# Weight sums moved from GpSimd to VectorE, and a source-ordered attention, in a one-layer transformer kernel

## Chip, cores and metric

The kernel runs as one program on 1 core of one Trainium2 chip. The metric is the device time of one execution in microseconds (us). Engines are named as in the profile: PE (TensorE matmul), PEld (its weight loads), DVE (VectorE), ACT (ScalarE), POOL (GpSimd), SP (SyncE, which here issues most DMAs).

## What is computed

One layer (DEPTH = 1), 2048 tokens, width 1024, 16 heads of 64, a feed-forward width of 2816, all in float32. Cut to what matters:

```python
def chunk_relpos_attention(h, w_qkv, w_o, rel_bias):       # chunks of 64 tokens
    q, k, v = split_heads(h, w_qkv)
    for c in range(n_chunks):                              # keys: own chunk and the 8 before it
        sc = einsum('bhqd,bhkd->bhqk', q_blk, k[:, :, k0:k1]) * scale + bias
        p = softmax(sc)
        outs.append(einsum('bhqk,bhkd->bhqd', p, v[:, :, k0:k1]))
    return merge_heads(concatenate(outs)) @ w_o

def reference(x, ...):
    h = rms_norm(x, g_pre_mix);  m = chunk_relpos_attention(h, w_qkv, w_o, rel_bias)
    x = x + rms_norm(m, g_post_mix)
    h = rms_norm(x, g_pre_ffn)
    return x + rms_norm((silu(h @ w_gate) * (h @ w_up)) @ w_down, g_post_ffn)
```

## The kernel before

**Split products.** Every large product is made of three matmuls (`products`, L185 to L187): both factors are split into a high part, copied by ACT (L131, L341), and a low remainder, subtracted by DVE (L132, L342), and hi*hi, hi*lo and lo*hi are summed in PSUM. Each weight tile (128x1024) thus costs one ACT copy and one DVE subtraction before TensorE can use it.

**Seven products for eight.** Values, queries and keys, gate and up, and down multiply 2x2 blocks with seven block products (B11, B21, T1, T2, B22, T3, T4). Four of them need sums of weight blocks, S1 to S4. For the first of two groups of 1024 tokens the kernel forms these sums itself: `sum_` in `block_items` adds two raw weight tiles in place (L834) and stores the sum in DRAM (L835) for the second group. There are 68 such adds: 8 for the values and 16 for queries and keys in the first 290 us, 44 for gate and up after 1217 us. (The sums for the down projection are made by DMA alone, L773, behind them on POOL's queue.)

**Stages.** `project` makes values, then queries and keys, for group 0 and then group 1, after some warm-up matmuls on an identity tile (L1256). The attention follows, then the last quarter of the output projection, then gate/up and down for both groups.

**Attention.** Tokens go in four quarters of 512; in each, eight pairs of heads; in each pair, four blocks of 128 queries. One block is a slot `t` (0 to 127). The first quarter has no earlier keys (`prev` false, up to 4 key blocks); in the others a block reads five key blocks (640 keys). Slot `t` emits, in this order: if it starts a pair, `output` of the pair before (`po`, L558, then its split, L341 and L342); `transposed(t)` (for either head four PE transposes into a PSUM tile `tt`, L528, copied to `pT` by DVE for head 0, L531, and by ACT for head 1, L533); `ahead(t + 3)`, the scores three slots ahead (L493, L494 into the single PSUM tile `st`, then per head a DVE reduction with the bias, L502, and an ACT exponential, L506; then a DVE reciprocal, L510, and a POOL scaling, L513); `fill`, some steps of the output projection of the quarter before; and `fifth` (two PE transposes for the fifth key block, L542, and one ACT copy for both heads, L543). The tag `tt` has two buffers, and a slot with earlier keys takes three of them: head 0, head 1, fifth.

**Output projection.** `o_quarter` takes 256 columns of `w_o` at a time, a slab of two weight tiles. `take` fetches slabs (`fetch`: DMA and split at once), one ahead. A result is copied by ACT (`y`, L582) into a tile of the ring `io` (three buffers) and stored; its squares are summed (L252, L253).

**Side work.** `later` is a queue of small steps; `tick` runs some after each product step, by due costs. `behind(w, n, lag, load, use)` spreads n loads and uses, each use `lag` steps behind its load. It serves the sums of squares and the residual writes (`write`, L1125, L1128; loads into `io` and the ring `sc`).

**Order.** PE issues in source order everywhere (`manual_schedule`). The order on ACT, DVE, POOL and SP is made by the planner of the tile framework from the source's order and expected times.

Of the kernel before, what the change touches and what calls it, by code (L numbers as in the profile page):

```python
# [9 lines left out]
F32 = mybir.dt.float32  # L10
# [39 lines left out]
def trunk(  # L50
# [79 lines left out]
    def split_part(hi, lo, raw):  # L130
        act.activation(hi, raw, AF.Copy)  # L131
        dve.tensor_tensor(lo, raw, hi.bitcast(F32), op=ALU.subtract)  # L132

    def fetch():
        n = len(ready)
        if n == len(plan):
            return
        tiles = [w_tile(f"{n}_{c}") for c in range(2)]
        for c in range(2):
            here = slice(c * 1024, c * 1024 + 1024)  # L140
            if "fp" in phase:
                part = phase["fp"].tile([P, 1024], F32, tag="w4", name=f"raw_{n}_{c}", bufs=phase["w4"])
            else:
                part = phase["ap"].tile([P, 1024], F32, tag="raw", name=f"raw_{n}_{c}", bufs=2)
            sp.dma_start(part, plan[n][:, here])
            split_part(*tiles[c], part)
        ready.append(tiles)

    taken = [0]

# [13 lines left out]
        def lo(self, k, c=slice(0, 256)):  # L164
            return self.part(1, k, c)

    def take(ahead=True):

        n = taken[0]
        taken[0] += 1  # L170
        if len(ready) == n:
            fetch()
        if ahead:
            fetch()
        return Slab(ready[n])

    def dense_bank(n):
# [254 lines left out]
    class Attend:  # L432
# [45 lines left out]
        def scores(self, ib):  # L478
# [17 lines left out]
            for h in range(2):  # L496
                c0 = cuts[h][0]
                sc = ap.tile([P, 640], F32, tag="sc", name="sc", bufs=8)
                nmax = rows[:, 4 + h : 5 + h]
                t = self.bias[h]  # L500
                rev = t[:, n - 1 :: -1] if n == 640 else t[:, 0:n][:, ::-1]
                dve.tensor_tensor_reduce(  # L502
                    out=sc[:, :n], in0=st[:, c0 : c0 + n], in1=rev, scale=-1.0, scalar=3.0e38,
                    op0=ALU.add, op1=ALU.min, accum_out=nmax,
                )
                act.activation(  # L506
                    sc[:, :n], sc[:, :n], AF.Exp, bias=nmax, scale=-1.0, accum_out=rows[:, h : h + 1]
                )
                self.sc[ib, h] = sc
            dve.reciprocal(rows[:, 2:4], rows[:, 0:2])  # L510
            for h in range(2):
                sc = self.sc[ib, h]
# [32 lines left out]
        def output(self):  # L545
            n, p = self.n, self.p
            v = values[n, p // 2]
            terms = [(0, 4, 0, HALF)]
            for r in range(1, 5 if self.prev else 4):
                if self.prev:  # L550
                    terms.append((r, r - 1, 0, r * P))
                if r < 4:
                    terms.append((r, 4 + r, r * P, HALF))
            po = phase["psa"].tile([P, HALF], F32, tag="po", name="po", bufs=1)
            for m, (r, kb, c0, c1) in enumerate(terms):
                for h in range(2):
                    c = (p % 2) * P + h * 64
                    pe.matmul(  # L558
                        po[heads[h], c0:c1], v[:, kb, c : c + 64], self.pT[:, h, r, c0:c1],
                        start=m == 0, stop=m == len(terms) - 1,  # L560
                    )
            if p == 0:
                ats[n] = Cols(((0, 1), (2, 3))[n % 2])
            split(ats[n].hi(p), ats[n].lo(p), po)

    def o_quarter(n):

# [3 lines left out]
        for d2 in range(KT // 2):  # L571
# [3 lines left out]
            for dt in (2 * d2, 2 * d2 + 1):  # L575
                pt = dense_bank(dt)
                c = slice((dt % 2) * P, (dt % 2) * P + P)
                for k in range(KT):
                    products(pt, w.hi(k, c), w.lo(k, c), src.hi(k), src.lo(k), k == 0, k == KT - 1)
                    yield 3 * C512  # L580
                t = io("y")
                act.activation(t, pt, AF.Copy)  # L582
                sp.dma_start(o_d[n][:, dt, :], t)
# [2 lines left out]
    class Blocks:  # L586
# [8 lines left out]
        def sums(self, w, on_all=False):  # L595
# [4 lines left out]
            for t in range(2):  # L600
# [11 lines left out]
                        self.total = nrm_tile("total")  # L612
                    add_square(c.pop(k), self.total, k == 0)

                steps += behind(w, KT, 1, load, use)
                if on_all:
                    steps.append((0.0, lambda t=t: later.extendleft(reversed(root_steps(self.rows[t], 1.5)))))
                    continue
# [204 lines left out]
    def block_items(src, key, early=True, ahead=None):  # L823
# [7 lines left out]
                sp.dma_start(r[a], src[BLOCK_AT[a]])  # L831

        def sum_(name, to, a, b, op=ALU.add):
            pool.tensor_tensor(r[to], r[a], r[b], op=op)  # L834
            last_pool[0] = pool.dma_start(sums_d[key][name], r[to])  # L835

        def make(n):
# [246 lines left out]
    class Late:  # L1084
# [5 lines left out]
        def sums(self, w):  # L1090
# [8 lines left out]
                    self.total = nrm_tile("total")  # L1099
                add_square(c.pop(dt), self.total, dt == 0)  # L1100

            return behind(w, KT, 1, load, use)

        def rstd(self, wait):
            return [(0.0, lambda: later.extendleft(reversed(root_steps(self.total, wait))))]
# [9 lines left out]
        def write(self, w, eng=dve):  # L1115
# [12 lines left out]
                eng.tensor_tensor(y, res, y, op=ALU.add)  # L1128
                sp.dma_start(self.dst[:, dt, :], y)

            return behind(w, KT, 1, load, use)


    rs, rows_of = [], {}
# [117 lines left out]
    def project():  # L1252

        warm = ps.tile([P, HALF], F32, tag="mm", name="warm")
        for _ in range(9):
            pe.matmul(warm[:, 0:P], ident, ident, start=True, stop=True)  # L1256
        groups = [Blocks([x[2 * g + t] for t in range(2)], PRE_MIX, SLOTS[g]) for g in range(NG)]
        for g in range(NG):
# [260 lines left out]
    def ahead(t):  # L1519
        if t < slots:  # L1520
            jobs[t // 4].scores(t % 4)
            if t % 4 == 1 and t // 4 + 1 < len(jobs):
                jobs[t // 4 + 1].load()

    for t in range(AHEAD):
        ahead(t)
    for t in range(slots):
        share = (0.4 if t % 4 == 0 else 1.2) * left[0] / max(per - t % per - 1, 1)
        if t > 0 and t % 4 == 0:
            fill(0.45 * share)  # L1530
            jobs[t // 4 - 1].output()
            if t % per == 0:
                n = t // per - 1
                fill(1e9)
# [3 lines left out]
                    later.extend(lates[n - 1].rows(1.5) + lates[n - 1].write(3.0, pool))  # L1538
                if n == 2:
                    later.extend(blocks[0].sums(2.0))  # L1540
        job = jobs[t // 4]
        job.transposed(t % 4)
        ahead(t + AHEAD)
        fill((0.55 if t % 4 == 0 else 1.0) * share)
        job.fifth()
    jobs[-1].output()
    fill(1e9)
    drain()
    for _ in sums_:
        pass  # L1550
    stack_a.close()
# [87 lines left out]
```

## Time and profile before

| | |
|---|---|
| median of 3 runs | 2501.5 us (2500.98 to 2511.96) |
| the profiled execution | 2506.22 us, its span 2504.4 us |
| mean granted TensorE clock | 0.982 |
| busy: PE, DVE, ACT, POOL | 94%, 67%, 46%, 20% of the span |
| instructions | 33018 |

The profile describes one execution. The span runs from its first to its last instruction; times in rows are microseconds from the span's start. A busy share is a mean over stages with different limits. An entry such as "[0.37 <-DVE rows L502]" says that the engine was idle for 0.37 us before the instruction, and that DVE's write of `rows` at line 502 ended the wait.

### The profile page before, as it was taken

The numbers are of one execution on the slowest core, as the hardware profiler recorded it, in microseconds if no ns is written. First come the engines' busy times: TensorE is split into PE (matmuls) and PEld (weight loads), VectorE is DVE, ScalarE is ACT, GpSimd is POOL, SyncE is SP. The second block draws the span as 40 slices with busy tenths as digits, with TensorE's granted clock in tenths as the row PEclk, the third lists the DMA queues.
The fourth block names the chain that finished last, engine by engine and source line by source line (L and its number), as shares of the span: only waits on it lengthen the run. The fifth ranks groups of instructions, "written<-read, shape, count | busy, mean of one in ns | idle before, by whom it ended". The sixth has DMA issues, their size and how long they took to land.

```text
span 2504.4 us, 33018 instructions
## 1 busy us (share of the span) xinstructions
PE 2360.5 (94%) x11442; PEld 1914.6 (76%) x11442; DVE 1672.8 (67%) x2557; ACT 1162.8 (46%) x2039; POOL 498.2 (20%) x490
## 2 busy tenths in 40 slices
PE   7899999978888899898999999999999999999998
PEld 6677788856666677666888878888888888888887
DVE  8768856556555565566977687676657657555567
ACT  6443743346555565565532333355443333334454
POOL 4223012123332433431433233300000000000002
PEclk8999999989999999999999999999999999999999
DMA  6466789999767877784576654457765755547654
GB/s 252 161 228 215 250 240 325 298 240 258 215 169 194 244 201 204 227 230 156 185 249 222 219 180 156 151 202 226 235 237 170 249 182 190 175 146 246 193 188 153
DMA packets 229783, 529.73 MB, mean 212 GB/s; under 512 B 26320, under 2 KB 42720, under 8 KB 225136
## 3 DMA queue, kind: packets, MB, share of 16 engines
q1 hardware_dynamic: 217712, 480.42, 60.9%
q0 software_dynamic: 11904, 47.19, 6.2%
q8 instruction: 91, 1.49, 0.3%
q14 instruction: 76, 0.62, 0.1%
HBM read 380.14 MB, written 170.44 MB: 220 GB/s over the span
## 4 chain that ended last, share of the span: by engine, by line
PE 54%; DVE 2%; ACT 1%; issue 1%; DMA 0%; POOL 0%; DVEq 0%; SPq 0%; ACTq 0%
PE pd L187 6%; PE pd L185 6%; PE pd L186 6%; PE pb L186 4%; PE pb L187 4%; PE pb L185 4%; PE pc L186 3%; PE pc L187 3%; PE pc L185 3%; PE pa L185 3%; PE pa L186 3%; PE pa L187 3%; PE po L558 1%; PE mm L187 1%; PE mm L185 1%; PE mm L186 1%
## 5 line engine op out<-in xcount | busy, mean ns | idle before, releaser
L513 POOL TENSOR_SCALAR sc<-sc,rows 128x640 f32<-128x640 f32 (+4 forms) x256 | 194.7, 773 | 399.7 <-DVE rows L510 197.7
L834 POOL TENSOR_TENSOR raw<-raw,raw 128x1024 f32<-128x1024 f32 x68 | 179.9, 2646 | 394.3 <-DMA raw<-in_w_gu 139.6
L506 ACT ACTIVATE sc<-sc,rows 128x640 f32<-128x640 f32 (+4 forms) x256 | 192.9, 755 | 112.6 <-DVE rows L502 112.4
L502 DVE CUSTOM_DVE_ANT_0 sc<-st,bias 128x640 f32<-128x640 f32 (+2 forms) x248 | 176.0, 746 | 86.0 <-PE st L494 60.4
L185 PE MATMUL pb<-hb,w_wg_T 128*128 128x512 f32 x528 | 205.6, 389 | 0.0
L187 PE MATMUL pb<-hb,w_wg_T 128*128 128x512 f32 x528 | 205.4, 389 | 0.0
L186 PE MATMUL pb<-hb,w_wg_T 128*128 128x512 f32 x528 | 205.4, 389 | 0.0
L528 PE MATMUL tt<-ident,sc 128*128 128x128 f32 x928 | 140.6, 281 | 45.6 <-DVE pT L531 21.5
L277 POOL TENSOR_TENSOR rs<-ms,neg_half 128x4 f32<-128x4 f32 (+1 forms) x7 | 7.9, 1125 | 854.8 <-DVE ms L275 854.8
L528 PEld LDWEIGHTS tt<-ident,sc 128*128 128x128 f32 x928 | 105.0, 143 | 82.2 <-issue 72.1
L493 PE MATMUL st<-k,q 128*128 128x384 f32 (+3 forms) x440 | 140.7, 340 | 28.0 <-DVE rows L502 23.1
L187 PE MATMUL pd<-a,w_d_T 128*128 128x512 f32 (+1 forms) x368 | 139.8, 380 | 0.1
L185 PE MATMUL pa<-hb,w_wg_B 128*128 128x512 f32 x352 | 137.7, 391 | 2.4 <-ACT terms L922 2.4
L185 PE MATMUL pd<-a,w_d_T 128*128 128x512 f32 (+1 forms) x368 | 139.9, 380 | 0.0
L186 PE MATMUL pd<-a,w_d_T 128*128 128x512 f32 (+1 forms) x368 | 139.7, 380 | 0.0
L186 PE MATMUL pa<-hb,w_wg_B 128*128 128x512 f32 x352 | 137.7, 391 | 0.0
L187 PE MATMUL pa<-hb,w_wg_B 128*128 128x512 f32 x352 | 137.5, 391 | 0.0
L943 ACT ACTIVATE terms<-terms 128x512 f32<-128x512 f32 x65 | 41.1, 632 | 195.9 <-DVE terms L941 195.9
L494 PE MATMUL st<-k,q 128*128 128x384 f32 (+3 forms) x440 | 129.9, 315 | 0.0
L531 DVE COPY pT<-tt 128x512 f32<-128x512 f32 (+3 forms) x128 | 81.6, 637 | 69.6 <-ACT hb L341 36.2
L342 DVE TENSOR_TENSOR a<-raw_a,a 128x512 fp32r<-128x512 f32 x154 | 105.7, 694 | 30.1 <-ACT a L341 29.9
L558 PE MATMUL po<-pT,v 128*64 128x384 f32 (+3 forms) x864 | 125.2, 436 | 0.0
(265 smaller groups left out, 6343.6 us busy)
## 6 DMA issues: line engine op xcount, KB each, us to landing
raw<-in_w_gu SPq DMA_DIRECT2D x77, 512.0 KB, 4.1
q<-q SPq DMA_DIRECT2D x62, 512.0 KB, 6.7
k<-k SPq DMA_DIRECT2D x55, 512.0 KB, 9.2
s_g_S<-raw POOLq DMA_DIRECT2D x44, 512.0 KB, 3.1
raw_d<-d_S SPq DMA_DIRECT2D x88, 256.0 KB, 3.6
raw_a<-aT SPq DMA_DIRECT2D x88, 256.0 KB, 3.6
raw<-s_g_S SPq DMA_DIRECT2D x44, 512.0 KB, 3.8
bias<-ext_d SPq DMA_DIRECT2D x124, 144.0 KB, 9.2
```

The lines of the kernel that those rows point to most:

```text
L185: pe.matmul(pt, a_hi, b_hi, start=first, stop=False, skip_group_check=go_on)
L186: pe.matmul(pt, a_hi, b_lo, start=False, stop=False, skip_group_check=go_on)
L187: pe.matmul(pt, a_lo, b_hi, start=False, stop=last, skip_group_check=go_on)
L342: eng.tensor_tensor(lo, src, hi.bitcast(F32), op=ALU.subtract)
L493: pe.matmul(st[:, a:b], q[:, 2 * h, cols], kk[:, h, key], start=True, stop=False)
L494: pe.matmul(st[:, a:b], q[:, 2 * h + 1, cols], kk[:, h, key], start=False, stop=True)
L502: dve.tensor_tensor_reduce(out=sc[:, :n], in0=st[:, c0 : c0 + n], in1=rev, scale=-1.0, scalar=3.0e38, op0=ALU.add, op1=ALU.min, accum_out= ...
L506: act.activation(sc[:, :n], sc[:, :n], AF.Exp, bias=nmax, scale=-1.0, accum_out=rows[:, h : h + 1])
L513: last_pool[0] = pool.tensor_scalar(sc[:, :n], sc[:, :n], rows[:, 2 + h : 3 + h], 1.0, op0=ALU.mult, op1=ALU.mult)
L528: pe.transpose(tt[:, u, :], sc[h][:, b * P : b * P + P], ident)
L558: pe.matmul(po[heads[h], c0:c1], v[:, kb, c : c + 64], self.pT[:, h, r, c0:c1], start=m == 0, stop=m == len(terms) - 1,)
L834: pool.tensor_tensor(r[to], r[a], r[b], op=op)
```

## The change

The sums of weight blocks run on DVE. `fetch` only issues the DMAs, and a new function `part_split` splits one tile of a slab at fixed points. The reciprocal and the scaling (`scaled`) are emitted one slot later, ahead of the next scores. The DVE half of the split of `output` (`low`) is emitted after those scores. Sums of squares and residual writes (`Blocks.sums`, `Late.sums`, `Late.write`) load two steps ahead of their use, not one. The first matmuls on the identity are 28 for 9. In the attention ACT and DVE issue in the order in which the source emits. Line numbers of the profile are those of the kernel before.

```diff
+    raws = []
     def fetch():
-        n = len(ready)
+        n = len(raws)
...
             sp.dma_start(part, plan[n][:, here])
-            split_part(*tiles[c], part)
-        ready.append(tiles)
+            parts.append(part)
+        raws.append(parts)
+
+    def part_split(c):
+        n = len(ready) - (c > 0)
+        if n == len(raws):
+            return
+        if c == 0:
+            ready.append([w_tile(f"{n}_{i}") for i in range(2)])
+        split_part(*ready[n][c], raws[n][c])
...
-    def take(ahead=True):
+    def take():
...
+        if len(raws) == n:
+            fetch()
         if len(ready) == n:
-            fetch()
-        if ahead:
-            fetch()
+            part_split(0)
+            part_split(1)
+        fetch()
         return Slab(ready[n])
...
                 self.sc[ib, h] = sc
+            self.open = (ib, rows, n)
+
+        def scaled(self):
+            ib, rows, n = self.open
             dve.reciprocal(rows[:, 2:4], rows[:, 0:2])
...
-            split(ats[n].hi(p), ats[n].lo(p), po)
+            act.activation(ats[n].hi(p), po, AF.Copy)
+            return lambda: dve.tensor_tensor(ats[n].lo(p), po, ats[n].hi(p).bitcast(F32), op=ALU.subtract)
...
                     yield 3 * C512
+                    if k == 3 and len(ready) == taken[0] and dt % 2:
+                        part_split(0)
+                    elif k == KT - 2 and dt % 2 and len(ready) > taken[0]:
+                        part_split(1)
...
-                steps += behind(w, KT, 1, load, use)
+                steps += behind(w, KT, 2, load, use)
...
-            return behind(w, KT, 1, load, use)
+            return behind(w, KT, 2, load, use)
...
-            pool.tensor_tensor(r[to], r[a], r[b], op=op)
+            dve.tensor_tensor(r[to], r[a], r[b], op=op)
             last_pool[0] = pool.dma_start(sums_d[key][name], r[to])
...
-        for _ in range(9):
+        for _ in range(28):
             pe.matmul(warm[:, 0:P], ident, ident, start=True, stop=True)
...
+    order = ctx.enter_context(ExitStack())
+    order.enter_context(tc.manual_schedule(engines={mybir.EngineType.DVE, mybir.EngineType.Activation}))
     for t in range(AHEAD):
         ahead(t)
+        if t < AHEAD - 1:
+            jobs[0].scaled()
     for t in range(slots):
...
-            jobs[t // 4 - 1].output()
+            low = jobs[t // 4 - 1].output()
...
+        if t == 16:
+            fetch()
+        elif t in (20, 22):
+            part_split(t // 2 - 10)
         job = jobs[t // 4]
         job.transposed(t % 4)
+        if t + AHEAD - 1 < slots:
+            jobs[(t + AHEAD - 1) // 4].scaled()
         ahead(t + AHEAD)
+        if t > 0 and t % 4 == 0:
+            low()
         fill((0.55 if t % 4 == 0 else 1.0) * share)
         job.fifth()
-    jobs[-1].output()
+    jobs[-1].output()()
     fill(1e9)
     drain()
+    order.close()
```

More of the change, by code (lines that the diff above doesn't have):

```diff
@@ L132, in split_part @@
         dve.tensor_tensor(lo, raw, hi.bitcast(F32), op=ALU.subtract)
+    raws = []
     def fetch():
-        n = len(ready)
+        n = len(raws)
         if n == len(plan):
             return
-        tiles = [w_tile(f"{n}_{c}") for c in range(2)]
+        parts = []
         for c in range(2):
@@ L1129, in use @@
                 sp.dma_start(self.dst[:, dt, :], y)
-            return behind(w, KT, 1, load, use)
+            return behind(w, KT, 2, load, use)
     rs, rows_of = [], {}
```

## The prediction

> **What bounds the kernel now.** I read the page's first part, then the busy time by stage (windows cut at the stages' first matmuls), then TensorE's waits, then the timelines around the waits.
>
> ```profile
> PE 2360.5 (94%) x11442; PEld 1914.6 (76%) x11442; DVE 1672.8 (67%) x2557; ACT 1162.8 (46%) x2039; POOL 498.2 (20%) x490
> ...
> 10.20:80.10 69.90, 52.89 (x184) 39.40 (x185) 64.62 (x66) 49.62 (x82) 30.58 (x20) 0.79 0.56 217
> 118.90:289.70 170.80, 157.75 (x681) 128.76 (x681) 127.55 (x149) 81.57 (x122) 40.49 (x26) 0.98 0.70 236
> 289.70:365.90 76.20, 76.20 (x338) 63.12 (x337) 52.67 (x73) 40.21 (x58) 7.84 (x10) 1.00 0.73 212
> 365.90:518.30 152.40, 152.40 (x676) 126.25 (x674) 95.56 (x127) 53.39 (x72) 28.14 (x46) 1.00 0.98 300
> 622.00:1163.40 541.40, 483.29 (x3076) 372.26 (x3075) 316.35 (x665) 315.12 (x681) 182.31 (x207) 0.99 0.73 202
> 1217.50:1649.30 431.80, 425.49 (x1878) 351.12 (x1877) 327.12 (x372) 151.79 (x208) 135.04 (x84) 1.00 0.55 187
> ```
>
> Columns: window, length, then PE, PEld, DVE, ACT, POOL busy, granted clock, DMA share, GB/s. TensorE is the bound, and only its idle time can be won. The second group's projection (289.7 to 518.3) runs without a gap; the first group's, equal in products, has DVE at 92% in 10.2:80.1, a clock of 0.79, and 18.4 us more in queries and keys (170.8 against 152.4). The attention with prior keys (622.0:1163.4) leaves 58.1 us idle. The gate-up stage in which weights are still summed leaves 6.3.
>
> **1. Weight sums on VectorE.** 68 adds of 128x1024 leave POOL. Their group in the first 520 us, then rows of the timelines (start, length, engine, line, operation, tiles; in brackets the idle time before and what ended it):
>
> ```profile
> L834 POOL TENSOR_TENSOR raw<-raw,raw 128x1024 f32<-128x1024 f32 x24 | 61.0, 2542 | 111.7 <-DVE w_wq_B L132 53.7 <-DMA raw<-in_w_qk 29.7 <-DMA raw<-in_w_v 16.6
> ...
> 18.44 6.44 DVE L253 TENSOR_TENSOR total<-total,sq 128x512 f32<-128x512 f32 x2
> 24.80 6.65 DVE L342 TENSOR_TENSOR hb<-hb,hb 128x512 fp32r<-128x512 f32 x2
> 34.64 1.22 DVE L132 TENSOR_TENSOR w_wv_T<-raw,w_wv_T 128x1024 fp32r<-128x1024 f32 x1
> 37.80 8.35 DVE L132 TENSOR_TENSOR w_wv_T<-raw,w_wv_T 128x1024 fp32r<-128x1024 f32 x1
> ...
> 37.38 4.74 POOL L834 TENSOR_TENSOR raw<-raw,raw 128x1024 f32<-128x1024 f32 x2
> ...
> 148.97 2.72 DVE L423 SCALAR_TENSOR_TENSOR lo<-terms,hi 128x512 fp32r<-128x512 f32 x1 [0.70 <-ACT hi L422]
> 152.33 0.69 DVE L420 TENSOR_TENSOR terms<-terms,row 128x512 f32<-128x512 f32 x1
> ...
> 76.63 1.11 PE L337 MATMUL prs<-ident,hr 128*128 128x128 f32 x4 [9.63 <-POOL hr L1302]
> 155.51 0.47 PE L185 MATMUL pb<-hb,w_wq_T 128*128 128x512 f32 x1 [3.99 <-DVE terms L1224]
> ```
>
> The same subtraction takes 1.22 us alone and 8.35 us beside POOL's adds (two of them in 37.38 to 42.12, then a third). I price an add on DVE like that form, 1.22: 83 us for all 68, but the stalls go. To 46 us the three stretched rows hold (6.44 - 2 x 0.69) + (6.65 - 2 x 0.69) + (8.35 - 1.22) = 17.5 us of stall (0.69 by 152.33); the seven adds up to there cost 8.5 on DVE, so DVE is 9 us earlier. TensorE there waits for DVE, and then for the row of the second block at 76.63, whose four serial loads start when ScalarE, which waits for DVE, gets to them, as much earlier: **-9**. Ends: 0 (adds ahead of the operands) and -18. In queries and keys of group 0, 155.51 is late by stalls like 2.72 for 0.69; two adds cost 2.4 of each 3.7 saved, and TensorE's half-speed products after the wait go too. Of 18.4 us I take **-6** (0 to -14). Gate-up: 6.3 idle in all, **-4** (-6 to +4). What was POOL's own wait for a weight load (29.7 and 16.6 us in the first row) would now stand in VectorE's queue with all splits behind it; that is the third rival. The stores of the sums stay on POOL, behind adds that end earlier.
>
> **2. 28 warm-up products.** Their rows:
>
> ```profile
> 1.35 4.21 PE L1256 MATMUL warm<-ident 128*128 128x128 f32 x18 [1.35 <-POOL ident masks.py:199]
> 10.22 0.80 PE L185 MATMUL pv<-w_wv_B,hb 128*128 128x512 f32 x1 [4.66 <-ACT hb L341]
> ```
>
> Nine end at 5.56, and the first real product waits to 10.22. At that pace 28 take 4.21 x 28/9 = 13.1 us and end at 14.4, at most 4.2 too late, and less if the clock rises on the way. Further on TensorE waits for DVE (term 1) whenever it comes early, so this hides: **0** (-2 to +4, where it does not).
>
> **3. Slabs of the output projection split earlier.** TensorE's timeline, and one window for the clock:
>
> ```profile
> 630.44 0.61 PE L185 MATMUL mm<-hb,w 128*128 128x512 f32 x1 [3.73 <-ACT w L131]
> 1180.45 0.80 PE L185 MATMUL mm<-hb,w 128*128 128x512 f32 x1 [3.22 <-ACT w L131]
> 1183.47 0.80 PE L187 MATMUL mm<-hb,w 128*128 128x512 f32 x1 [1.79 <-DVE w L132]
> ...
> 613.60:617.00 3.40, 3.40 (x16) 3.25 (x15) 1.40 (x4) 1.01 (x3) 1.58 (x2) 0.50 1.04 219
> 613.38 0.45 PE L493 MATMUL st<-k,q 128*128 128x384 f32 x1 [1.90 <-DVE rows L502]
> ```
>
> Both waits are for the first slab of a pass. They go (8.7 us), and with each the half clock that follows (as after the 1.90 wait: 3.4 us at 0.50, so 1.7 lost; two such, 3.4). The first slab's two halves (1.22 on DVE each, 1.06 on ACT by the row of part 5) move into slots 20 and 22, where no product covers them: +2.5. Next late is the chain of part 5. **-10**. The loads go one slab earlier through SP into two buffers that the previous split has freed; SP gains no instruction. Ends -12 and -3.
>
> **4. Lag 2, and reciprocals later.** Rows of VectorE and TensorE in the last quarter of the attention:
>
> ```profile
> 1035.83 0.75 DVE L1125 SCALAR_TENSOR_TENSOR y<-y,gt,osum 128x512 f32<-128x512 f32 x1 [1.51 <-DMA y<-o]
> 1038.12 0.69 PE L493 MATMUL st<-k,q 128*128 128x384 f32 x1 [2.60 <-DVE rows L502]
> ```
>
> VectorE's wait for a load held the reductions and cost 2.60 and a half clock. A second load ahead removes it, but three `res` tiles now hold all three `io` buffers, so the projection's `y` copy can wait on ScalarE for POOL's add: **-4** (-8 to +6). The reciprocal no longer follows its exponentials at once; POOL's scaling has two slots to spare: 0.
>
> **5. Source order on ScalarE and VectorE.** Rows of the first block (slot) of a pair by engine, of the same slot in another pair, and the group of these transposes over 622.0:1163.4:
>
> ```profile
> 720.49 0.34 PE L494 MATMUL st<-k,q 128*128 128x384 f32 x1
> 720.67 0.38 PE L542 MATMUL tt<-ident,sc 128*128 128x128 f32 x2
> 720.88 1.36 PE L528 MATMUL tt<-ident,sc 128*128 128x128 f32 x8
> 722.61 0.44 PE L493 MATMUL st<-k,q 128*128 128x384 f32 x1 [0.37 <-DVE rows L502]
> ...
> 721.08 0.38 ACT L543 ACTIVATE pT<-tt 128x256 f32<-128x256 f32 x1 [0.74 <-PE tt L542]
> 722.67 0.82 ACT L506 ACTIVATE sc<-sc,rows 128x640 f32<-128x640 f32 x1
> 661.45 1.06 ACT L131 ACTIVATE w<-raw 128x1024 fp32r<-128x1024 f32 x1 [1.28 <-PE mm L187]
> 726.69 0.36 ACT L543 ACTIVATE pT<-tt 128x256 f32<-128x256 f32 x1
> 727.20 0.63 PE L528 MATMUL tt<-ident,sc 128*128 128x128 f32 x4 [0.45 <-ACT pT L543]
> ...
> 721.73 0.82 DVE L502 CUSTOM_DVE_ANT_0 sc<-st,bias 128x640 f32<-128x640 f32 x1
> 722.47 0.69 DVE L531 COPY pT<-tt 128x512 f32<-128x512 f32 x1
> ...
> 651.40 0.34 PE L494 MATMUL st<-k,q 128*128 128x384 f32 x1
> 654.21 0.63 PE L528 MATMUL tt<-ident,sc 128*128 128x128 f32 x4 [1.12 <-DVE pT L531]
> ...
> L528 PE MATMUL tt<-ident,sc 128*128 128x128 f32 x763 | 113.7, 277 | 45.6 <-DVE pT L531 21.5 <-ACT pT L543 13.8 <-DVE rows L510 6.3
> ```
>
> A slot takes three `tt` buffers out of two. The second transposes of the next slot need the copy of `fifth` (L543) or VectorE's copy of their own first half. Here L543 ran at 721.08, ahead of the exponentials, and eight transposes followed at once. In source order `fifth` comes after the exponentials: scores end at 720.83 (S), the second exponential at 723.49, then L543 (0.36): S + 3.0. VectorE is no earlier: reductions end S + 1.7, then the deferred `low` (0.69, by its form), the copy (0.69): S + 3.1. So these transposes start at S + 3.2, and the next scores 0.4 later: S + 3.6, against S + 1.8 here (722.61) and S + 2.9 in the other kind (S 651.74, transposes 654.21, scores 0.4 later), where one step of three products lies between. The slots between have this order already (726.69, 727.20). Of 24 pairs I counted 16 of the first kind and 6 of the second: 16 x 1.8 + 6 x 0.7 = **+33**. The ends: 0, if something fills the hole, and +43 (24 x 1.8).
>
> Behind it: slab halves and `y` copies now always run after the exponentials, 1.06 us ahead of `fifth`, where before some lay in the shadow of the reductions: **+8** (0 to +20): of 24 halves and 24 copies I count a third with no `po` products over them, at half of 1.06. The first quarter, without products: the copy of the last block waits for two exponentials, +0.2 a pair, **+2**. Holes of 2.5 us: the 1.90 wait above was followed by half clock. If a quarter of 16 do so at 1.7 us: **+6** (0 to +27).
>
> The Trainium skill ("TensorE: Matmul & The Clock Gate", section "HAM oscillation — how this bites in real kernels") asks only for no idle gaps over about 3.4 us. By it the clock term would be 0 and the time 2511. The trace disagrees: 613.60:617.00 shows 0.50 after a gap of 1.90.
>
> **The sum**, against the profiled execution's own 2506.2 us (span 2504.4; 4.7 above the median of 2501.5): -9 - 6 - 4 + 0 - 10 - 4 + 33 + 8 + 2 + 6 = +16. From the median: **2517 us**.
>
> **The rivals.**
> A, faster: the order costs nothing, because it leaves TensorE free to take projection products into the hole, or does not bind as written. Then +49 goes: 2501.5 - 33 = 2468. For it: projection products are at hand in every quarter but the first. Against: TensorE's own order is written out, and the slots between wait in exactly this way.
> B, a draw: part 5 holds and the start gains twice as much (-18 and -13, both near their ends): 2501. For it: DVE at 64.62 of 69.90 us there. Against: the row at 76.63 waits for four loads one after the other.
> C, worse: VectorE stands for weight loads. From POOL's 46 us of such waits in the projection, a fifth comes through (9), and part 1's gain of 19 goes with it: 2517 + 19 + 9 = 2545. Against: VectorE's queue there is filled by expected readiness.
> D, the clock rule: holes without half clock, 2511, told from the forecast only by the clock after them.
>
> **How the numbers follow.** 0.5% is 12.5 us, about what a measurement here can tell from no change. Forecast 0.36 (own range 2503 to 2540, 0.30 of it above 2514), A 0.28, B 0.16 (0.10 within, 0.06 faster), C 0.10, D 0.10 (0.06 within, 0.04 above). Faster 0.34, within 0.22, slower 0.44. The range takes in half of A and most of C: 2466 to 2545.
>
> **What would show it.** Right: L834 on DVE near 1.2 us and no DVE subtraction over 3 us before 50 us; the row wait of 76.63 about 9 us earlier; no wait at the first slab; in each pair's first slot L543 after both exponentials and a TensorE wait of about 2.5 us before the second transposes, so that 622:1163 grows by some 35 us. Wrong: the waits before L528 in the attention below 45.6 us in total, or products between scores and these transposes; or VectorE waiting on weight loads.

## The result, and the profile after

The changed kernel takes 2547.0 us (median; 2541.5 to 2550.9) against 2503.4 for the kernel before on the same chip: a ratio of 1.0166, 95% interval 1.0135 to 1.0198. It is slower, by 44 us where 16 were forecast. In us that is 2 above the top of the range; the range was laid out from 2501.5 us, though, and as a ratio its top is 2545 / 2501.5 = 1.0174, so 1.0166 lies just inside it.

The profiled execution took 2550.9 us, its span is 2549.0; it is the longest of the four. Three views carry the reading. Busy time by engine, then the stages (window, length, then busy time and count on PE, PEld, DVE, ACT, POOL, granted clock, DMA share, GB/s); line numbers are now the changed kernel's, 12 to 22 higher.

```profile
PE 2377.4 (93%) x11480; PEld 1932.1 (76%) x11480; DVE 1627.7 (64%) x2625; ACT 1164.1 (46%) x2039; POOL 304.2 (12%) x422
...
10.50:101.30 90.80, 82.89 (x355) 66.94 (x354) 79.20 (x107) 63.17 (x100) 8.85 (x14) 0.96 0.64 239
101.30:261.30 160.00, 155.94 (x682) 127.92 (x682) 121.25 (x161) 82.69 (x122) 8.59 (x14) 0.99 0.75 252
490.20:608.60 118.40, 86.36 (x475) 64.14 (x474) 66.20 (x229) 65.61 (x191) 39.53 (x72) 0.84 0.96 243
608.60:1211.20 602.60, 497.26 (x3048) 384.49 (x3047) 289.84 (x655) 311.02 (x670) 168.18 (x203) 0.95 0.64 179
```

The same stages of the kernel before: values of group 0, the first quarter of the attention, its other three quarters. (The prediction shows queries and keys, 118.90 to 289.70.)

```profile
10.20:118.90 108.70, 91.69 (x353) 71.50 (x354) 90.42 (x97) 64.51 (x100) 39.50 (x26) 0.86 0.53 200
518.10:630.40 112.30, 81.61 (x475) 61.66 (x473) 66.79 (x232) 67.51 (x195) 40.35 (x73) 0.91 0.96 251
630.40:1163.40 533.00, 479.08 (x3047) 368.86 (x3048) 311.06 (x652) 309.10 (x668) 178.55 (x203) 0.99 0.73 202
```

The attention starts at 490.2 us where it started at 518.1: the projection is 27.9 us shorter. The attention takes 721.0 us (490.2 to 1211.2) for 645.3: 75.7 more. What follows takes 1337.8 for 1341.0. Together -27.9 + 75.7 - 3.2 = +44.6, the difference of the two spans. Nearly all of the loss lies in quarters 2 to 4, +69.6. Length less PE busy gives the idle time there: 105.3 us for 53.9. The other 18 us are in the busy time itself: as many products (3048 and 3047) take 497 us for 479, and the granted clock fell from 0.99 to 0.95.

TensorE's waits in the changed kernel (who waited, for whom: us in total, times, longest):

```profile
PE tt L545 <- ACT pT L560: 87.4, 53, 3.0
...
PE mm L197 <- ACT w L131: 2.7, 1, 2.7
PE pb L197 <- DVE terms L963: 3.2, 2, 2.9
```

The first row is the wait that the prediction named: the transposes for `fifth`'s copy (L543 before, L560 now), 87.4 us. The second is what is left of the waits for a first slab (one, in the last pass), the third the feed-forward's. It is in the first slot of a pair that one sees why. PE and ACT on the timeline (start, length, in brackets the idle time before and what ended it):

```profile
702.49 0.34 PE L506 MATMUL st<-k,q 128*128 128x384 f32 x1
702.67 0.38 PE L559 MATMUL tt<-ident,sc 128*128 128x128 f32 x2
...
703.84 0.83 ACT L518 ACTIVATE sc<-sc,rows 128x640 f32<-128x640 f32 x1 [1.50 <-DVE rows L514]
...
704.67 0.81 ACT L518 ACTIVATE sc<-sc,rows 128x640 f32<-128x640 f32 x1
...
705.48 0.36 ACT L560 ACTIVATE pT<-tt 128x256 f32<-128x256 f32 x1
705.99 0.63 PE L545 MATMUL tt<-ident,sc 128*128 128x128 f32 x4 [2.50 <-ACT pT L560]
706.37 0.42 PE L505 MATMUL st<-k,q 128*128 128x384 f32 x1
...
707.63 0.52 PE L506 MATMUL st<-k,q 128*128 128x384 f32 x1
```

Scores end at 702.83 (S). `fifth`'s transposes are done at 703.05, and ScalarE is idle then until 703.84, yet the copy L560 stands behind both exponentials and ends at 705.84. The second transposes follow at S + 3.16, the next scores at S + 3.54; the prediction had S + 3.2 and S + 3.6. A moment later the same score product takes 0.52 for 0.34: the window 707.30 to 710.60 has a granted clock of 0.50.

The start went as foretold in kind, and further in size. DVE's timeline, the group of the sums and what they waited for (us in all, times), and two rows of TensorE:

```profile
31.04 2.35 DVE L132 TENSOR_TENSOR w_wv_T<-raw,w_wv_T 128x1024 fp32r<-128x1024 f32 x2
...
L856 DVE TENSOR_TENSOR raw<-raw,raw x68: 1214/1219/1227, 19.4 to 1655.1; 128x1024 f32<-128x1024 f32 x68
  DMA raw<-in_w_gu: 1.5, 3
...
1.35 9.43 PE L1278 MATMUL warm<-ident 128*128 128x128 f32 x56 [1.35 <-POOL ident masks.py:199]
61.38 0.65 PE L349 MATMUL prs<-ident,hr 128*128 128x128 f32 x4 [1.27 <-POOL hr L1324]
```

An add takes 1.22 us on DVE, and the subtraction that had taken 8.35 beside POOL's adds takes its 1.2 again (two in 2.35). DVE stood 1.5 us in all ahead of these sums for weight loads. The row wait of 9.63 at 76.63 is one of 1.27 at 61.38.

### The profile page after: what moved, and what is told of

The parts are those of the page before. It is cut to its first block, busy times and chain, and to the rows that moved or that the text cites. A ratio compares the mean times of both kernels' runs of the same rounds, so it can differ in the third digit from the quotient of the medians.

```text
span 2549.0 us, 33018 instructions
## 1 busy us (share of the span) xinstructions
PE 2377.4 (93%) x11480; PEld 1932.1 (76%) x11480; DVE 1627.7 (64%) x2625; ACT 1164.1 (46%) x2039; POOL 304.2 (12%) x422
## 4 chain that ended last, share of the span: by engine, by line
PE 55%; DVE 3%; ACT 3%; issue 2%; DMA 2%; POOL 1%; SPq 0%; DVEq 0%; POOLq 0%; ACTq 0%
PE pd L199 5%; PE pd L197 5%; PE pd L198 5%; PE pb L197 4%; PE pb L199 4%; PE pb L198 4%; PE pc L197 3%; PE pc L199 3%; PE pc L198 3%; PE pa L197 3%; PE pa L198 3%; PE pa L199 3%; PE po L575 2%; ACT sc L518 2%; PE tt L545 1%
## 5 line engine op out<-in xcount | busy, mean ns | idle before, releaser
L545 PE MATMUL tt<-ident,sc 128*128 128x128 f32 x928 | 146.8, 289 | 104.6 <-ACT pT L560 87.4
L530 POOL TENSOR_SCALAR sc<-sc,rows 128x640 f32<-128x640 f32 (+4 forms) x256 | 184.5, 733 | 454.1 <-DVE rows L527 315.2
L545 PEld LDWEIGHTS tt<-ident,sc 128*128 128x128 f32 x928 | 108.0, 147 | 144.4 <-issue 141.1
L505 PE MATMUL st<-k,q 128*128 128x384 f32 (+3 forms) x440 | 148.3, 356 | 18.7 <-DVE rows L514 12.0
L506 PE MATMUL st<-k,q 128*128 128x384 f32 (+3 forms) x440 | 137.4, 331 | 0.0
L575 PE MATMUL po<-pT,v 128*64 128x256 f32 (+3 forms) x864 | 129.7, 450 | 6.1 <-ACT pT L560 6.1
L131 ACT ACTIVATE w_wg_T<-raw 128x1024 fp32r<-128x1024 f32 x88 | 92.9, 1057 | 72.5 <-PE pa L199 31.2
L197 PEld LDWEIGHTS pb<-hb,w_wg_T 128*128 128x128 f32 x528 | 99.6, 189 | 25.4 <-issue 4.4
```

Of the source, the lines that this page charges most:

```text
L197: pe.matmul(pt, a_hi, b_hi, start=first, stop=False, skip_group_check=go_on)
L505: pe.matmul(st[:, a:b], q[:, 2 * h, cols], kk[:, h, key], start=True, stop=False)
L506: pe.matmul(st[:, a:b], q[:, 2 * h + 1, cols], kk[:, h, key], start=False, stop=True)
L530: last_pool[0] = pool.tensor_scalar(sc[:, :n], sc[:, :n], rows[:, 2 + h : 3 + h], 1.0, op0=ALU.mult, op1=ALU.mult)
L545: pe.transpose(tt[:, u, :], sc[h][:, b * P : b * P + P], ident)
L575: pe.matmul(po[heads[h], c0:c1], v[:, kb, c : c + 64], self.pT[:, h, r, c0:c1], start=m == 0, stop=m == len(terms) - 1,)
```

## The experiments

Twelve kernels ran. The theory after the result (T1): the source order puts `fifth`'s copy behind the exponentials, the next transposes wait for its buffer, and the holes bring half clock. The rivals: another part of the order (T2), or the slabs and lag 2 (T3). "Change" means the changed kernel. Ratios are to the kernel before.

**e1, the order taken away.**

```diff
-    order.enter_context(tc.manual_schedule(engines={DVE, Activation}))
```

> The changed kernel with only the source order of ScalarE and VectorE in the attention taken away again; all other parts stay. Theory T1 (the attention's 76 us come from the source order: in each pair's first slot the second transposes wait for fifth's copy behind both exponentials, and half clock follows the hole): the attention from first score to its end comes back from 721 to 645 to 660 us, the total is 2547 - 60 to 76 = 2471 to 2487, that is below the 2503 of the kernel before by the 28 us that the projection gained, and the waits of L545 for ScalarE's pT fall from 87 to below 25 us. Rival T2 (it is the order, but another part of it: weight splits and y copies in the queue) gives the same here and parts from T1 in e2 and e3. Rival T3 (lag 2, the slabs' fixed places, the later reciprocal make the attention longer, whoever orders): 2530 to 2550.

Measured: 2478.4 us, ratio 0.9895 (0.9878 to 0.9911). Quarters 2 to 4:

```profile
606.80:1136.70 529.90, 476.21 (x3048) 366.99 (x3047) 311.18 (x655) 310.29 (x671) 179.25 (x205) 1.00 0.73 202
```

602.6 us become 529.9, the clock is 1.00 again, idle 53.7. One line of the change, the order, costs 69 us; all the rest gains 27. T3 is out.

**e2, `fifth` ahead of the exponentials in each pair's first slot**, source order kept. TensorE's order hardly changes: only the products of that slot now stand behind `fifth`'s transposes.

```diff
 def scores(self, ib, between=None):
 ...                              # the score matmuls
+            if between is not None:
+                between()        # job.fifth, in slots with t % 4 == 0
 ...                              # reductions and exponentials
```

> The changed kernel, source order kept, but in each pair's first slot fifth (its two transposes and its ScalarE copy) is emitted between the score products and the reductions and exponentials, so that ScalarE has that copy ahead of the exponentials; the other three slots of a pair are as in the changed kernel. T1: 24 holes of 1.8 to 2.5 us close (24 x 1.8 = 43) and with them most of the twenty windows of half clock (1.7 each, 20 to 30 in all): 2547 - 40 to 65 = 2482 to 2507; first slots go from score end to score end in about 3.3 us instead of 4.9. T2: the splits and y copies in the queues stay where they are, so 2540 to 2550, and another wait takes the place of the one removed.

Measured: 2502.7 us, ratio 0.9993 (0.9983 to 1.0002).

```profile
607.00:1163.60 556.60, 485.97 (x3048) 371.28 (x3047) 290.52 (x655) 311.26 (x671) 171.21 (x205) 0.98 0.69 193
```

46 us shorter than in the change: idle 70.6 for 105.3 (34.7 less), busy 11.3 less. Where a copy stands in one slot of four was worth 44 us. T1 holds, but 26.7 us are left over e1's 529.9, and T1 as I had it, with the first slots alone, doesn't say why. Counted on TensorE's timeline from the end of the scores that a slot emits to the end of the next slot's, the first slots now take 13.5 us less in all than e1's; the two slots behind them take 18.3 more and the last slots of the pairs 19.8 more. Of those last slots two take 17.0 and 17.4 us, where none of e1's takes over 9.0: in its fixed place ahead of `fifth`'s copy, ScalarE's square waits for a store there, 5.72 us in the one and 6.30 in the other.

**e5, `fifth` ahead in every slot.** The same edit without the condition on the slot.

> As the kernel with fifth ahead of the exponentials in a pair's first slot, but now in every slot. What e2 left (attention 671 us against 647 without the source order) is, by my reading, weight splits of 1.06 us and y copies that ScalarE issues between the exponentials and fifth: slots with a split are 5.9 apart, those without 4.7 to 4.95, and some 20 waits of 1.35 us stand before the second transposes in slots that carry a split. With fifth ahead in all slots these waits go: 2503 - 15 to 28 = 2475 to 2488, attention 643 to 656. Rival (it is the splits on VectorE or the low part that hold the reductions, and fifth's place in these slots does not matter): 2497 to 2505.

Measured: 2456.0 us, ratio 0.9809 (0.9789 to 0.9828), 19 us below the expected range.

```profile
602.30:1115.60 513.30, 477.27 (x3048) 365.30 (x3046) 287.80 (x655) 314.41 (x671) 171.00 (x205) 0.98 0.75 209
```

Another 43.3 us. The other slots weren't free: in the order "exponentials, side work, `fifth`" a slot with a slab half mostly takes 5.9 us from score end to score end and one without 4.7 to 4.95; with `fifth` ahead most take 3.7 to 4.4, halves or none. The kernel before had lost time there too (4.7 to 5.6 in most).

**e10, `fifth` ahead in every slot, and no source order.**

> The changed kernel with fifth ahead of the exponentials in every slot, but without the source order on ScalarE and VectorE, so that the planner may place its copy where it likes. With both, the time is 2456.0; with neither, 2478.4. If the gain of 22 comes from TensorE's order alone (fifth's transposes come earlier there): 2452 to 2460. If it needs the source order, which puts the copy first on ScalarE in every slot: 2468 to 2480.

Measured: 2432.7 us, ratio 0.9713 (0.9696 to 0.9730), below both readings that I had offered, and the fastest of all. It beats the kernel before by 72 us and the changed one by 114.

```profile
600.90:1088.60 487.70, 473.15 (x3048) 368.02 (x3046) 299.37 (x655) 311.50 (x671) 190.54 (x205) 0.99 0.79 219
```

TensorE is idle for 14.6 of these 487.7 us. A first slot of this kernel:

```profile
678.40 0.38 PE L561 MATMUL tt<-ident,sc 128*128 128x128 f32 x2
678.62 1.36 PE L547 MATMUL tt<-ident,sc 128*128 128x128 f32 x8
678.82 0.38 ACT L562 ACTIVATE pT<-tt 128x256 f32<-128x256 f32 x1 [0.75 <-PE tt L561]
...
679.92 0.83 ACT L520 ACTIVATE sc<-sc,rows 128x640 f32<-128x640 f32 x1 [0.73 <-DVE rows L516]
```

The copy starts as its transposes end, in the time in which ScalarE waits for VectorE's reduction anyway, and all eight transposes of the next slot pass without a wait. So the four kernels give both factors in quarters 2 to 4: the source order costs 72.7 us with `fifth` late (602.6 against 529.9) and 25.6 with `fifth` early (513.3 against 487.7); `fifth` early gains 42.2 without the order. What the order costs beside `fifth` shows in e5's waits (rows under e11). This kernel still has lag 2; with lag 1 it was not run.

**e6, the hole filled with useless work.** In the change, the four transposes of head 0 are done three times (eight more) in each pair's second slot, ahead of those that wait.

```diff
-                for u, (r, b) in enumerate(part):
+                for u, (r, b) in list(enumerate(part)) * (3 if h == 0 and ib == 1 and self.prev else 1):
```

> The changed kernel with the eight... four transposes of head 0 done three times over (the same values again) in the second slot of each pair with earlier keys, right before the second transposes that wait: 24 x 8 products more that nobody needs, 0.16 us each, 1.26 us of TensorE work in each hole of 1.8 to 2.5 us. The wait for fifth's copy ends when it did, so nothing is won by order; what is left of a hole is 0.5 to 1.2 us. If the half clock (19 windows in the attention, 22.9 us by which the same products take longer than before) comes from the holes: fewer than 8 windows after 605 us and 2547 - 10 to 22 = 2525 to 2537. If the half clock has another cause: 2547 to 2560 with as many windows. Against both, VectorE's copy of head 0 comes 1.26 us later, and where it becomes the last, up to 24 x 0.5 = 12 are added.

Measured: 2540.0 us, ratio 1.0140 (1.0120 to 1.0160). Quarters 2 to 4, and one of the holes:

```profile
611.00:1203.20 592.20, 502.56 (x3232) 390.16 (x3230) 289.89 (x655) 310.66 (x670) 168.88 (x203) 0.98 0.64 182
...
654.29 1.47 PE L545 MATMUL tt<-ident,sc 128*128 128x128 f32 x12
657.39 0.63 PE L545 MATMUL tt<-ident,sc 128*128 128x128 f32 x4 [1.63 <-ACT pT L560]
```

The hole is 1.63 us for 2.50, and the clock 0.98 for 0.95; by the trace's clock record the windows of half clock in these quarters fall from 14 to 6. By the two rows eight useless transposes add 1.47 - 0.63 = 0.84 us, 20 in 24 pairs, so the useful products take about 502.6 - 20 = 482 for 497, 15 us less. The clock record agrees: half clock lasts 23.9 us in these quarters for 54.6, which at half speed is 15 us. So most of the half clock came from the holes. But the stage is only 10.4 us shorter, above the 2525 to 2537 that this reading expected, and the total 7, with intervals that overlap those of the change (1.0135 to 1.0198). Of the clock's 15 us some 10 were time. VectorE's later copy of head 0 took little of the rest: without half clock a first slot takes 4.99 us on average, for 4.95 in the change. My reading, not shown apart, is that where the wait for ScalarE sets the pace faster products only wait longer.

**e7, real products in the hole.** Shares of a pair's four slots 1.3, 1.2, 1.0, 0.5 for 0.4, 1.2, 1.2, 1.2, the first slot's all behind its scores.

```diff
-        share = (0.4 if t % 4 == 0 else 1.2) * left[0] / ...
+        share = (1.3, 1.2, 1.0, 0.5)[t % 4] * left[0] / ...
-            fill(0.45 * share)
-        fill((0.55 if t % 4 == 0 else 1.0) * share)
+        fill(share)
```

> The changed kernel, order kept, with the projection's products handed out otherwise: the slots of a pair take shares of 1.3, 1.2, 1.0, 0.5 for 0.4, 1.2, 1.2, 1.2, and the first slot's all lie after the scores, so that about four steps of three products (0.7 us each) stand in the hole. Rival A of the prediction (products can fill the hole) with the wait left where it is: the first slot still takes 4.9 us, but 0.9 of the share, about two steps or 1.3 us a pair, is gone from the last slot: 24 x 1.3 = 31, and with the holes the half clock, 10 to 20: 2547 - 31 to 51 = 2496 to 2516. If the last slot, which carries the output products, has a chain of its own that the products hid, only half of it: 2520 to 2530. If the hole does not cost what I say: 2540 to 2550.

Measured: 2537.9 us, ratio 1.0141 (1.0115 to 1.0168): 9 us for an expected 31 to 51, with an interval that overlaps the change's. A miss. ScalarE and TensorE in such a first slot:

```profile
655.76 0.81 ACT L518 ACTIVATE sc<-sc,rows 128x640 f32<-128x640 f32 x1
656.57 1.04 ACT L131 ACTIVATE w<-raw 128x1024 fp32r<-128x1024 f32 x1
657.52 0.58 ACT L604 ACTIVATE y<-mm 128x512 f32<-128x512 f32 x1
658.00 0.58 ACT L264 ACTIVATE sq<-mm 128x512 f32<-128x512 f32 x1
658.47 0.38 ACT L560 ACTIVATE pT<-tt 128x256 f32<-128x256 f32 x1
659.00 0.63 PE L545 MATMUL tt<-ident,sc 128*128 128x128 f32 x4 [3.03 <-ACT pT L560]
```

The products bring their side work along: slab half, `y` copy and square are emitted with them, and in source order they stand on ScalarE between the exponentials and `fifth`. The copy ends at 658.85, 2.28 us behind the second exponential's end. This wait grew to 3.03 us; all the waits of L545 for that copy come to 85.1 us, for 87.4 in the change.

**e3, another buffer for `fifth`.** It takes its PSUM tile from the ring of the projection's products.

```diff
-            tt = phase["psa"].tile([P, 4, P], F32, tag="tt", name="tt", bufs=2)    # in fifth
+            tt = norm_bank("tt5")
```

> The changed kernel, source order kept, but fifth takes its PSUM tile from the ring of the projection's products and not from the two buffers of tt, so that a slot needs two tt buffers and the next slot's second transposes wait for copies that ended earlier. T1: all waits of L545 for fifth's copy go, in every slot: 2547 - 45 to 75 = 2472 to 2502, unless the ring of the projection's products becomes the wait (then a wait of mm or pt for L560 appears, and the gain shrinks to 0 to 30). T2: 2535 to 2550.

Measured: 2545.4 us, ratio 1.0163 (1.0148 to 1.0178): no gain.

```profile
PE tt L559 <- ACT sq L264: 54.1, 18, 6.6
```

`fifth` now waits for the square of a projection result, which frees that ring: 54.1 us in 18 waits. The expectation had allowed for that ring, though not for this row. The test says nothing on T1; it swapped one late copy on ScalarE for another.

**e4 and e9, the sums alone.** The kernel before with the sums on VectorE and 28 warm-up products (e4), or 9 (e9).

```diff
-            pool.tensor_tensor(r[to], r[a], r[b], op=op)
+            dve.tensor_tensor(r[to], r[a], r[b], op=op)
-        for _ in range(9):                                   # e4 alone
+        for _ in range(28):
```

> The kernel before with two parts of the change alone: weight sums on VectorE and 28 warm-up products. If the projection's 28 us come from VectorE no longer being held up by GpSimd's adds: 2503 - 24 to 32 = 2471 to 2479, with values of group 0 at about 91 us and queries and keys at 160. Rival (the 28 us come from elsewhere, for instance other order of the queues by the planner with the whole change): 2490 to 2503. The attention stays at 645 us in both.

> The kernel before with the weight sums on VectorE and still 9 warm-up products; with 28 the same kernel stood at 2471.7. If the warm-up is worth nothing, as I predicted (0, -2 to +4): 2468 to 2474. If more products at the start matter, because the first products then run at the full clock: 2474 to 2484, the loss before 100 us.

Measured: e4 2471.7 us, ratio 0.9868 (0.9853 to 0.9883); e9 2469.0, ratio 0.9856 (0.9841 to 0.9871). The sums are worth 34 to 36 us, 28 to 29 of it ahead of the attention (which starts at 490.4 and 489.3) and some 5 behind it. The warm-up is worth nothing.

**e8, e4 with lag 2.**

```diff
-                steps += behind(w, KT, 1, load, use)         # and two more places
+                steps += behind(w, KT, 2, load, use)
```

> The kernel before with weight sums on VectorE, 28 warm-up products, and now lag 2 in the sums of squares and the residual writes. Without lag 2 this stood at 2471.7, and the changed kernel without its source order at 2478.4; lag 2, the slabs' fixed places and the later reciprocals therefore cost 6.7 together. If lag 2 is the cost (three res tiles take all io buffers; feed-forward 1268 to 1270 in all kernels with lag 2 against 1265.0 without): 2474 to 2479, 3 to 4 of it after the attention. If it is the slabs: 2469 to 2473. If lag 2 wins its 4 us as I predicted: 2466 to 2469.

Measured: 2480.5 us, ratio 0.9901 (0.9883 to 0.9919): 8 us slower than e4, the ends of the intervals touching. The profiled executions lie further apart, 12.7 us in their spans. Of these, 4.9 lie behind the attention, where a wait stands (first row, e8) that e4 has at 0.3 (second row):

```profile
PE pb L185 <- DVE terms L941: 3.3, 2, 3.0
```

```profile
PE pb L185 <- DVE terms L941: 0.3, 1, 0.3
```

The other 8.3 lie in the attention (652.1 us for 643.8; e9 has 643.5), nearly all in quarters 2 to 4 (537.8 for 529.0), and I can't say for what reason. e8 and e1 differ by the slabs' fixed places, the later reciprocals and the later `low`; 0.9901 and 0.9895 are the same, so these are worth nothing that shows.

**e11 and e12, lag 1 and later halves with `fifth` ahead and source order.** e11 is e5 with lag 1; e12 also emits the halves of slots 20 and 22 behind that slot's exponentials. The lines below are e12's alone.

```diff
-        elif t in (20, 22):
-            part_split(t // 2 - 10)
 ...
         ahead(t + AHEAD, job.fifth if early else None)
+        if t in (20, 22):
+            part_split(t // 2 - 10)
```

> The kernel with source order and fifth ahead in all slots, with lag 1 for 2 in the sums of squares and residual writes. There the waits of fifth's transposes for ScalarE's copy of head 1 (25.3 us, 13 times, up to 6.5) stand in pairs in which ScalarE waits for a tile that the residual writes hold (sq behind y, 9.5 us once). With lag 1 fewer tiles are held: 2456 - 6 to 14 = 2442 to 2450, and 3 of it after the attention. If lag 1 brings VectorE's waits for loads into the fixed order (as the 2.60 and 1.51 of the kernel before): 2452 to 2462.

> As the one with lag 1, and the two slab halves of slots 20 and 22 are emitted behind that slot's exponentials instead of ahead of its transposes. In the pair around 557 us the halves cost 6.5 us more than a pair without them (predicted: 2.5 for both): ScalarE's 1.06 and VectorE's 1.22, which waits for it, run one after the other ahead of the copies that the scores wait for. Behind the exponentials they have one slot of slack: 3 to 6 us less than lag 1 alone. If the place doesn't matter: the same within 2.

Measured: 2456.6 us, ratio 0.9805 (0.9785 to 0.9825), and 2459.4, ratio 0.9813 (0.9797 to 0.9828); e5 had 0.9809. Neither moves the time. What e5's TensorE and ScalarE wait for (ScalarE's row in quarters 2 to 4):

```profile
PE tt L561 <- ACT pT L552: 25.3, 13, 6.5
ACT sq L264 <- DMA x<-y: 19.4, 3, 9.5
```

The same of e11, with VectorE:

```profile
PE tt L547 <- DVE rows L529: 10.9, 4, 5.2
DVE y L1149 <- DMA y<-o: 18.7, 2, 9.7
```

With lag 2, ScalarE's square stands in its fixed place until the store of a residual write has freed a tile, up to 9.5 us, and the copy of head 1 behind it; with lag 1, VectorE stands as long for the load of one, and the reciprocals behind it. That is the case for which the expectation gave 2452 to 2462. In e10, without the order, VectorE's longest wait of this kind is 1.8 us, and ScalarE's square waits 0.9 at most for a DMA. By these rows such waits are what the order costs beside `fifth`; no run takes them alone away. The place of the two halves is of no account; why the pair with the halves takes 6.5 us more stays open.

## Why the prediction was right, and where not

**The mechanism and the sign were right.** The hole is where part 5 put it, as long as it said (twelve waits of 2.50 us), and by its chain: S + 3.54 for S + 3.6. Closing it (e2) takes 34.7 us of idle time away; the term was +33.

**The order's other terms were too small.** It costs 73.2 us over the whole attention (721.0 against e1's 647.8, 117.9 + 529.9) where 33 + 8 + 2 + 6 = 49 stood. Where it lies shows from score end to score end, slot by slot, in quarters 2 to 4 of the change and of e1.

- The first slots, with the hole, take 122.6 us in all for 88.7: 33.9 more. Where no half clock falls into them a slot takes 4.95 on average for 3.77, which over the 23 in the stretch is 27 us where 33 stood; half clock brings the rest.
- The two slots behind each take 255.4 for 233.1: 22.3 more, and in e2, with hardly any half clock there, still 18.3. The step that failed is this one: "a third with no `po` products over them, at half of 1.06", +8. Of these 46 slots 16 hold a slab half, and all those without half clock but two take 5.9 us, against 5.0 on average without a half. Behind the exponentials a half stands ahead of `fifth`'s copy, and the next slot waits for that. Only beside the output products, where six more stand, does a half hide (8.95 to 8.98 in e1 too).
- The last slots, with those output products, take 214.0 for 202.0, and for these 12.0 us nothing stood. Three of them take 10.2, 11.7 and 15.3, where e1's longest takes 9.0. In the longest, ScalarE's square waits for the store of a residual write, and `fifth`'s copy behind it:

```profile
1079.56 0.60 ACT L264 ACTIVATE sq<-mm 128x512 f32<-128x512 f32 x1 [4.16 <-DMA x<-y]
1080.05 0.38 ACT L560 ACTIVATE pT<-tt 128x256 f32<-128x256 f32 x1
```

The remaining 5 lie in the first quarter and at the ends of the stretch. I also wrote that the slots between "have this order already" and left them at nothing; that they had it was true, but it had been costing time all along (e10: 42 us against e1).

**The half clock was under-sized.** +6 stood, from a quarter of 16 holes. Quarters 2 to 4 have 14 windows of half clock against 2 before, and products run 21 us longer than in e1 (497.3 against 476.2). Of the 18 waits of 2.1 to 3.0 us before L545 there, 12 have the start of a window of half clock within 1.5 us of their end; of the 10 of 1.7 to 1.9, none; in e6, where twelve are 1.63, none. So the rate was two in three. e6 also shows a thing that the term had not in it: not all of this is time (10.4 of the 15 us there).

**Rival D is out.** The Trainium skill ("TensorE: Matmul & The Clock Gate", section "HAM oscillation — how this bites in real kernels") asks for no idle gaps over about 3.4 us. The trace disagrees, now by an experiment: the longest of the waits in question is 3.0, and windows of half clock fall from 14 to 6 when 2.5 becomes 1.63.

**Terms 1 and 2.** The projection gained 27.9, not 15. The idle time fell as the terms said: in values by 9.1 (17.0 to 7.9), in queries and keys by 9.0 (13.05 by the prediction's row, to 4.1). What was not in them is the clock: the same products in values took 91.69 us before at 0.86 and take 82.89 at 0.96. By the clock record half clock lasts 30.7 us there before and 6.8 in the change. Fewer waits, another 8.8, and part of it the warm-up's: the first such window is 10.2 us long with nine warm-up products (before, e9) and 3.4 with 28 (the change, e4), though e4 and e9 take the same time. I had the two half-speed products after each wait in mind for queries and keys alone. This comes near rival B's condition (both terms near their ends), and a draw would have followed had the order cost 49. The warm-up's 0 stands (e9). Rival C has no ground: 1.5 us of waits for loads ahead of the sums.

**Terms 3 and 4.** -10 and -4 stood; nothing and +8 came. The first slab's wait at 630 is gone, but the one in the last pass is there still (2.7, in the waits above). e1 and e8 show no gain from the slabs, and lag 2 costs about 8 (e8 against e4). That is past my end of +6. Some of it (4.9 of the 12.7 in the profiled executions) lies behind the attention, where I hadn't looked. The first quarter is 6 us longer (118.4 for 112.3; +2 stood), but two kernels with the same attention give 111.8 and 114.8 (e9, e4), and the change's without the order 117.9 or 112.1 (e1, e10), so that isn't settled.

**Rival A is out.** Without the order the time is 2478, near its 2468, but A said that the order costs nothing, and it costs 69 us: it binds as written, and the products that e7 put into the hole brought side work that made the wait no shorter.

**The sum.** Forecast against traces: projection -15 and -27.9; attention with order +35 (33 + 8 + 2 + 6 - 10 - 4, the -10 counted here whole, though one of its two waits stands behind the attention) and +75.7; the rest -4 and -3.2. The errors of the first two had opposite signs, 13 and 41.

## What to carry to other kernels

When an engine's order is written out, look first for its short instructions that free a buffer of a small ring, and put them ahead of the long ones: a copy of 0.36 us behind two exponentials, in one slot of four, cost this kernel more than all its moved sums had won (44 us by e2, 34 to 36). Look, too, for what waits for a DMA in that order: the traces here show it holding everything behind it for up to 9.7 us. Price idle holes of TensorE together with the clock after them, but do not count on getting all of that back where another engine's chain sets the pace. And test a change of several parts one part at a time: here one part was worth -34 us, one +69, one +8, and the best version (e10) drops one part of the change and adds an edit that it did not contain.

## What the runs showed of the hardware that I had not expected

In the attention of the change, half clock followed two in three of TensorE's waits of 2.1 to 3.0 us before L545 and none of its ten of 1.7 to 1.9; none of e6's twelve of 1.63 was followed by it. It is no sharp threshold over the whole trace: the prediction shows one behind 1.90, and the last window of the attention follows waits of 1.43 and 0.69. One that follows a hole of 2.50 (at 705.99 above):

```profile
707.30:710.60 3.30, 3.30 (x11) 2.72 (x10) 1.58 (x4) 1.45 (x3) 0.27 (x1) 0.50 1.02 218
```

Such a window is 3.41 us long by the clock record, or twice that (two of the change's 14). In values, where the mean clock is 0.86 before and 0.96 in the change, half clock lasts 30.7 us before: 10.2 around the end of a wait of 4.66, 10.2 from inside the one of 9.63, and 10.2 in two pieces behind waits of 0.9 to 2.3. In the change it lasts 6.8.

And the sums cost DVE nothing in the end: with the sums alone (e9) its busy time over the whole kernel is 1648.4 us for 1672.8, although it took over 68 adds of 1.22 (83 us). Its own instructions no longer stand stretched: the subtraction of a weight tile for the values takes 1.22 us at most in the start of the change, where one took 8.35 beside POOL's adds. (The change's 1627.7 has a further part that is not the sums': in quarters 2 to 4 DVE's busy time is 289.8 us with the source order and 311.2 without, e1.)
